# Order of two attentions in an encoder layer, and attention scores on row halves

## The chip, the cores and the metric

One core of a Trainium2 chip runs the whole kernel. The metric is the device time of one execution in microseconds. TensorE (PE) does the matrix products and transposes, its weight loads stand apart as PEld, VectorE is DVE, ScalarE is ACT, GpSimd is POOL, SyncE (SP) issues the transfers.

## The reference

One hybrid encoder layer on 256 rows of width 2048, all in fp32. A vector `c` gives shift, scale and gate for a mixer and a feed-forward part (`mod = silu(c) @ w_ada`). The mixer projects the modulated norm of x once; its columns feed two groups of eight heads, whose outputs are concatenated and projected.

```python
# differential attention: two maps of 64 per head, values of 128
s = einsum('bqhcd,bkhcd->bhcqk', q * 64 ** -0.5, k)
p = softmax(s)
out_d = einsum('bhqk,bkhe->bqhe', p[:, :, 0] - lam * p[:, :, 1], v)   # then RMSNorm per head
# latent attention: q and (k, v) projected up from latents of 512 and 256
s = (einsum('bqhd,bkhd->bhqk', q_nope, k_nope)        # 128 per head
     + einsum('bqhr,bkr->bhqk', q_rope, k_rope)) * 192 ** -0.5   # 64, one key for all heads
out_m = einsum('bhqk,bkhe->bqhe', softmax(s), v)
x = x + gate * (concat(out_d, out_m) @ w_out)
```

The feed-forward part (hidden width 8192, squared ReLU) and a last norm follow; the change leaves both as they are.

## The kernel before

**Products.** Every weight of the projections is loaded as fp32 in pieces of 128 rows by 1024 columns and split into two fp32r tiles: `split` casts the high half on ACT (L123) and subtracts it on DVE for the low half (L124). A product is then three matmuls (high by high, high by low, low by high) of 512 columns in `block` (L309). Raw weights have a ring of five buffers, their halves one of four. Scores, probabilities and transposes are single fp32 products.

**Modulation.** `w_ada` is applied on the side, in units: DVE multiplies a piece into an accumulator, two steps per MB (L376); some pieces go to PE instead, as four column tiles (L392). A run of the program takes a given number of units (the table `NA_`).

**Streams.** The program is written as generators, and `run` interleaves them by the weights of the table `RW`; a scheduler then fixes the order of each engine, which runs its instructions in that order. PSUM has eight banks: four for the projections ("mm"), a ring of three for attention ("at"), one for the gate groups.

**Order around the change.** The input projection ends with a last group of four k-tiles in four parts (latents, values, queries, keys of the differential heads). Beside its last two parts runs the first head pair's latent projection (`latent_kv`, L552 `pk` and `pv`; `latent_q`, `pq` and `pr`, with a swap product for the rotary halves). Then comes `attention`, alone with 18 units of modulation: for each head the latent scores (`ms`), the differential heads' transposes (`dT`, L664) and scores (`ds`, L677), and two heads later the transposes of the probabilities (`mtp`, `dtp`) and the outputs (`mo`, `do`). Then follow the latent half of the output projection's first 1024 columns with four units, the norm of the differential heads (`diff_norm`, L710 to L718: clamp, square, row sum, product) and their transposes (`oT`, L725), the differential half (`od`) of these columns, and the second 1024 columns.

**Scores.** A head's two maps of 64 rows share the 128 partitions. The keys are copied into a tile with zeros in the other half (`kz`), so that one 128-row product of 512 columns gives both maps' scores for 128 queries. The latent rotary part has its keys zero-padded in the same way (`krz`). Scores go into "mm" banks. The softmax takes the row maximum on DVE (L603), scales it (L604), and exponentiates on ACT with the scale (L606); reciprocals of the row sums multiply the probabilities.

Of the kernel before, what the change touches and what calls it, by code (L numbers as in the profile page):

```python
# [11 lines left out]
F32 = mybir.dt.float32  # L12
# [43 lines left out]
NA_ = (0, 2, 5, 18, 4, 2, 0)  # L56
PRI_ADA = 0
RW = (11.9, 5.6, 0.5, 2.88, 1.44, 28.56, 13.6, 6.8, 336.0, 45.0, 42.0, 3.53, 60.48, 6.0)
FW = (42.0, 2.0, 2, 2)
PRI_ATT = 0  # L60

TWO_PI = 2.0 * np.pi
# [22 lines left out]
def encoder_layer(ctx: ExitStack, tc: tile.TileContext, x, c, positions, w_ada, b_ada, g_norm_mix, w_in,  # L85
# [41 lines left out]
    def splits(w, raw, name, ext):  # L127
        if not ext:
            return [split([P, w], raw[:, i, :], f"{name}{i}") for i in range(2)]
        hi = act.tile([P, 2, w], F32R, tag="n0", name=name + "_hi")  # L130
        lo = act.tile([P, 2, w], F32R, tag="n1", name=name + "_lo")
# [364 lines left out]
    krz = mla_g[:, 512:1024].rearrange("p (a q) -> p a q", a=2)  # L496
# [11 lines left out]
    def latent_prep():  # L508
        g.memset(krz, 0.0)
# [33 lines left out]
        v.tensor_tensor(krz[0:64, 0, :], t1[0:64, :], t2[0:64, :], ALU.add)  # L543
        v.tensor_tensor(krz[64:128, 1, :], t1[64:128, :], t2[64:128, :], ALU.add)
# [10 lines left out]
    def latent_kv(hp):  # L555
# [8 lines left out]
        s.copy(kn[hp % 2], pk.rearrange("p (h q) -> p h q", h=2))  # L564
# [9 lines left out]
    def latent_q(hp, hold):  # L574
# [24 lines left out]
        hold.append((qn, qr))  # L599

    def softmax_rows(sc, scale, p, sums, name):
        nm = small.tile([P, 2], F32, tag="nm", name=name + "_nm")
        v.tensor_reduce(nm, sc, AX.X, ALU.max, negate=True)  # L603
        v.tensor_scalar(nm, nm, scale, None, op0=ALU.mult)  # L604
        for i in range(2):
            s.activation(p[:, i, :], sc[:, i, :], AF.Exp, bias=nm[:, i:i + 1], scale=scale,  # L606
                         accum_out=sums[:, i:i + 1])
        v.reciprocal(sums, sums)

    def latent_scores(h, qn, qr):  # L610
        i = h % 2
        kh = kn[h // 2 % 2][:, i, :]
        sc = bank(f"ms{h}", "mm")
        for t in range(T):
            pe.matmul(sc[:, t * S:(t + 1) * S], lhsT=qn[:, i, t * P:(t + 1) * P], rhs=kh, start=True, stop=False)
            pe.matmul(sc[:, t * S:(t + 1) * S], lhsT=qr[:, t * P:(t + 1) * P], rhs=krz[:, i, :],
                      start=False, stop=True)
        p = p_buf()
        sums = small.tile([P, 2], F32, tag="sums", name=f"msum{h}")
        softmax_rows(sc.rearrange("p (t k) -> p t k", t=2), float((NOPE + ROPE) ** -0.5), p, sums, f"m{h}")  # L620
        for t in range(T):
            s.mul(p[:, t, :], p[:, t, :], sums[:, t:t + 1])
        return p
# [36 lines left out]
    def diff_heads_T(h):  # L660
# [5 lines left out]
        qT = at.tile([P, S], F32, tag="dqT", name=f"dqT{h}", bufs=2)  # L666
        s.copy(qT, pt[:, 0:S])
        z = kz[h % 2]
        s.copy(z[0:64, 0, :], pt[0:64, S:2 * S])
        v.tensor_copy(z[64:128, 1, :], pt[64:128, S:2 * S])  # L670
        return qT, z

    def diff_scores(h, qT, z):
        ps = []
        for t in range(T):
            sc = bank(f"ds{h}{t}", "mm")
            pe.matmul(sc, lhsT=qT[:, t * P:(t + 1) * P], rhs=z.rearrange("p a b -> p (a b)"), start=True, stop=True)  # L677
            p = p_buf()
            sums = small.tile([P, 2], F32, tag="sums", name=f"dsum{h}{t}")
            softmax_rows(sc.rearrange("p (t k) -> p t k", t=2), float(DH ** -0.5), p, sums, f"d{h}{t}")  # L680
            v.tensor_tensor(sums[:, 1:2], sums[:, 1:2], nlam, ALU.mult)
            s.mul(p[:, 0, :], p[:, 0, :], sums[:, 0:1])
            v.scalar_tensor_tensor(p[:, 0, :], p[:, 1, :], sums[:, 1:2], p[:, 0, :], op0=ALU.mult, op1=ALU.add)
            ps.append(p)
        return ps
# [363 lines left out]
```

## Time and profile before

| | us |
|---|---|
| median of 3 runs (lowest, highest) | 1185.48 (1183.98, 1187.21) |
| the profiled execution | 1184.91 |
| its span | 1183.1 |
| PE busy in the span | 1139.7 (96%) |
| DVE busy | 810.0 (68%) |
| ACT busy | 552.4 (47%) |
| POOL busy | 53.3 (5%) |

The span is what the profiler saw, the time includes what lies around it. Busy shares are means over stages that differ: the attention stage lies between about 226 and 372 us, where single fp32 products and small steps take the place of long rows of fp32r products. A busy time per instruction can overlap the next one's on PE, so a price is better read from start to start. The mean granted clock of TensorE in this execution is .993 of 2.4 GHz.

### The profile page before, as it was taken

To read this page: it belongs to the slowest core of one execution; us is meant where nothing else is said; L and a number is where in the kernel's file an instruction comes from. 1 tells how busy PE (TensorE), PEld (TensorE's weight loads), DVE (VectorE), ACT (ScalarE), POOL (GpSimd) and SP (SyncE) were. 2 spreads that over 40 slices of the span, in tenths; PEclk is the share of its full clock that TensorE was granted. 3 is DMA by queue.
4 is the path that set the end of the run, shared out by engine and by line. 5 is a ranking of instruction groups with operands and counts; after the bars stand their busy time and mean duration, and the time that the engine had idled before them with its cause. 6 is when DMAs were issued, how large, how long until landed. Compare 5 with 4: busy or idle time off the path is not lost.

```text
span 1183.1 us, 14211 instructions
## 1 busy us (share of the span) xinstructions
PE 1139.7 (96%) x5502; PEld 913.8 (77%) x5502; DVE 810.0 (68%) x1012; ACT 552.4 (47%) x811; POOL 53.3 (5%) x50
## 2 busy tenths in 40 slices
PE   5999999998999998999999999999999999999996
PEld 4566778865778886888888888888888888888875
DVE  3245559996899869775754666676686676555776
ACT  3432334547774436545545444344344344344343
POOL 1000000112101000000000000000020002000000
PEclk9999999999999999999999999999999999999999
DMA  9999974786788877995565646667868767556531
GB/s 347 393 390 369 359 302 131 258 308 215 294 307 300 300 276 275 356 329 194 184 225 179 204 158 207 232 236 263 278 220 277 280 241 249 183 181 203 183 104 72
DMA packets 94196, 297.50 MB, mean 251 GB/s; under 512 B 5712, under 2 KB 16167, under 8 KB 93488
## 3 DMA queue, kind: packets, MB, share of 16 engines
q1 hardware_dynamic: 94016, 296.56, 71.3%
q8 instruction: 43, 0.70, 0.2%
q14 instruction: 25, 0.20, 0.0%
q10 hardware_dynamic: 112, 0.03, 0.0%
HBM read 294.47 MB, written 2.10 MB: 251 GB/s over the span
## 4 chain that ended last, share of the span: by engine, by line
PE 59%; DVE 1%; issue 1%; ACT 0%; ACTq 0%; POOLq 0%; POOL 0%
PE f_p L309 51%; PE f1a_p L309 7%; PE fT L936 1%; DVE x_res L954 0%; DVE acc L953 0%; DVE acc L951 0%; PE shift_f_pc L417 0%; PE scale_f_pc L417 0%; PE h2T L889 0%; ACT acc L885 0%; DVE acc L957 0%; ACT sq L960 0%; PE h2a L858 0%; ACT h2a10t L831 0%; ACT acc L981 0%
## 5 line engine op out<-in xcount | busy, mean ns | idle before, releaser
L124 DVE TENSOR_TENSOR f_w_lo<-f_r,f_w_hi 128x1024 fp32r<-128x1024 f32 x224 | 277.2, 1245 | 200.9 <-ACT f_w_hi L123 200.8
L123 ACT CAST f_w_hi<-f_r 128x1024 fp32r<-128x1024 f32 x224 | 236.2, 1054 | 317.6 <-PE f_p L309 300.3
L309 PE MATMUL f_p<-f_w_hi,h 128*128 128x512 f32 x768 | 209.5, 391 | 0.0
L309 PEld LDWEIGHTS f_p<-f_w_hi,h 128*128 128x128 f32 x768 | 143.4, 188 | 29.3 <-ACT h L892 0.2
L309 PE MATMUL f_p<-f_w_lo,fh 128*128 128x512 f32 x512 | 158.9, 389 | 0.0
L309 PE MATMUL f_p<-f_w_hi,fh 128*128 128x512 f32 x512 | 158.5, 390 | 0.3 <-ACT fh L938 0.3
L309 PE MATMUL f_p<-f_w_hi,fl 128*128 128x512 f32 x512 | 158.7, 389 | 0.0
L309 PE MATMUL in_p<-in_w_hi,hT 128*128 128x512 f32 (+1 forms) x512 | 140.8, 388 | 4.6 <-ACT hT L364 2.8
L309 PE MATMUL f_p<-f_w_lo,h 128*128 128x512 f32 x384 | 118.9, 390 | 0.0
L309 PEld LDWEIGHTS in_p<-in_w_hi,hT 128*128 128x128 f32 x512 | 95.0, 189 | 29.0 <-ACT in_w_hi L123 6.3
L309 PEld LDWEIGHTS f_p<-f_w_hi,fh 128*128 128x128 f32 x512 | 96.0, 188 | 21.6 <-DVE acc L951 1.2
L309 PEld LDWEIGHTS f_p<-f_w_hi,fl 128*128 128x128 f32 x512 | 96.0, 188 | 20.0
L309 PEld LDWEIGHTS f_p<-f_w_lo,fh 128*128 128x128 f32 x512 | 96.1, 188 | 19.7
L124 DVE TENSOR_TENSOR in_w_lo<-in_r,in_w_hi 128x1024 fp32r<-128x1024 f32 (+1 forms) x64 | 73.2, 1169 | 45.1 <-ACT in_w_hi L123 44.9
L309 PEld LDWEIGHTS f_p<-f_w_lo,h 128*128 128x128 f32 x384 | 72.0, 188 | 14.8
L309 PE MATMUL in_p<-in_w_lo,hT 128*128 128x512 f32 (+1 forms) x256 | 78.8, 386 | 1.7 <-DVE in_w_lo L124 1.5
L123 ACT CAST in_w_hi<-in_r 128x1024 fp32r<-128x1024 f32 (+1 forms) x64 | 62.8, 1010 | 37.0 <-PE in_p L309 27.4
L309 PE MATMUL f1a_p<-f1a_w_hi,h 128*128 128x512 f32 x256 | 69.4, 391 | 3.0 <-ACT h L863 3.0
L309 PEld LDWEIGHTS f1a_p<-f1a_w_hi,h 128*128 128x128 f32 x256 | 47.8, 188 | 14.0 <-ACT h L863 3.9
L309 PEld LDWEIGHTS in_p<-in_w_lo,hT 128*128 128x128 f32 x256 | 47.7, 189 | 12.2 <-DVE in_w_lo L124 5.1
L123 ACT CAST out_w_hi<-out_r 128x1024 fp32r<-128x1024 f32 x30 | 31.6, 1052 | 35.7 <-PE out_p L309 35.7
L376 DVE SCALAR_TENSOR_TENSOR gate_f<-gate_f_r,cs,gate_f 128x1024 f32<-128x1024 f32 x32 | 40.9, 1280 | 7.0 <-DMA gate_f_r<-w_ada 6.9
(341 smaller groups left out, 1374.9 us busy)
## 6 DMA issues: line engine op xcount, KB each, us to landing
f_r<-w_ff SPq DMA_DIRECT2D x112, 1024.0 KB, 5.6
in_r<-w_in SPq DMA_DIRECT2D x24, 1024.0 KB, 9.9
sc__r<-w_ada SPq DMA_DIRECT2D x16, 1024.0 KB, 12.1
sh__r<-w_ada SPq DMA_DIRECT2D x16, 1024.0 KB, 13.4
gate_m_r<-w_ada SPq DMA_DIRECT2D x16, 1024.0 KB, 6.8
scale_f_r<-w_ada SPq DMA_DIRECT2D x16, 1024.0 KB, 8.0
out_r<-w_out SPq DMA_DIRECT2D x16, 1024.0 KB, 7.6
shift_f_r<-w_ada SPq DMA_DIRECT2D x16, 1024.0 KB, 7.9
```

Of the source, the lines that this page charges most:

```text
L123: s.copy(hi, src)
L124: v.tensor_tensor(lo, src, hi.bitcast(F32), ALU.subtract)
L309: pe.matmul(ps[t][j][:, 0:nw], lhsT=lhs[(lk0 + kk) // 8][:, (lk0 + kk) % 8, t * P:(t + 1) * P], rhs=rhs[:, n0:n0 + nw], start=(kk == 0 and ...
L376: v.scalar_tensor_tensor(acc, raw[:, i, :], cs[:, k + i:k + i + 1], acc, op0=ALU.mult, op1=ALU.add)
L936: pe.transpose(pt[:, i * S + t * P:i * S + (t + 1) * P], rl[:, t, (kp + i) * P:(kp + i + 1) * P], ident)
```

## The change

- Latent attention of all four head pairs (`latent_attention`, with a pair's output one pair later) runs beside the last two parts of the input projection, with 17 units of modulation.
- Differential attention (`diff_attention`) runs beside the latent half of the output projection's first 1024 columns, with 5 units. The norm is split in two halves of four heads: the first stands behind head 3's output, within that stage, the second behind the stage. The split results `od` get tiles of their own, and the residual's rows are loaded earlier.
- Scores are products of 64 rows: the two heads of a latent pair and the two maps of a differential head take partitions 0 to 63 and 64 to 127 of the same tiles, with no zero padding. A differential head issues four products of 256 columns in place of two of 512. Scores go into the ring of three banks.
- The softmax scale is folded into the copies of keys and queries. The first map's row sum is kept (`s0_all`) and put into the norm, instead of dividing each map.

```diff
-NA_ = (0, 2, 5, 18, 4, 2, 0)
+NA_ = (0, 2, 17, 5, 0, 2)
...
-        s.copy(kn[hp % 2], pk.rearrange("p (h q) -> p h q", h=2))
+        s.mul(kn[hp % 2], pk.rearrange("p (h q) -> p h q", h=2), MLA_SCALE)
...
+    def softmax_rows(sc, p, sums, name):
         nm = small.tile([P, 2], F32, tag="nm", name=name + "_nm")
         v.tensor_reduce(nm, sc, AX.X, ALU.max, negate=True)
-        v.tensor_scalar(nm, nm, scale, None, op0=ALU.mult)
...
+    def latent_scores(hp):
+        qn, qr = hold[hp]
+        scs = [bank(f"ms{2 * hp + i}") for i in range(2)]
+        for t in range(T):
+            for i in range(2):
+                hs = slice(64 * i, 64 * i + 64)
+                pe.matmul(scs[i][:, t * S:(t + 1) * S], lhsT=qr[hs, t * P:(t + 1) * P], rhs=kr[hs, :],
+                          start=True, stop=False)
+            for i in range(2):
+                pe.matmul(scs[i][:, t * S:(t + 1) * S], lhsT=qn[:, i, t * P:(t + 1) * P], rhs=kn[hp % 2][:, i, :],
+                          start=False, stop=True)
...
+    def diff_scores(h, qkT):
+        scs = [bank(f"ds{h}{c_}") for c_ in range(2)]
+        for t in range(T):
+            for c_ in range(2):
+                hs = slice(64 * c_, 64 * c_ + 64)
+                pe.matmul(scs[c_][:, t * S:(t + 1) * S], lhsT=qkT[hs, 0, t * P:(t + 1) * P], rhs=qkT[hs, 1, :],
+                          start=True, stop=True)
+        ps = [p_buf(), p_buf()]
+        s0 = s0_all[:, h, :]
+        s1 = small.tile([P, 2], F32, tag="sums", name=f"dsum{h}")
+        for c_, sm in enumerate((s0, s1)):
+            softmax_rows(scs[c_].rearrange("p (t k) -> p t k", t=2), ps[c_], sm, f"d{h}{c_}")
+        v.reciprocal(s1, s1)
+        v.scalar_tensor_tensor(s1, s1, nlam, s0, op0=ALU.mult, op1=ALU.mult)
+        for t in range(T):
+            v.scalar_tensor_tensor(ps[0][:, t, :], ps[1][:, t, :], s1[:, t:t + 1], ps[0][:, t, :],
+                                   op0=ALU.mult, op1=ALU.add)
...
-    def diff_norm():
-        for t in range(T):
-            o_ = qk[t][:, 0:1024]
+    def diff_norm(part):
+        hs = slice(part * HQ, (part + 1) * HQ)
+        for t in range(T):
+            o_ = qk[t][:, part * 512:(part + 1) * 512]
...
+    def latent_attention():
+        for hp in range(H // 2 + 1):
+            if hp < H // 2:
+                yield from latent_kv(hp)
+                yield from latent_q(hp)
+            for h in (2 * hp - 2, 2 * hp - 1):
+                if h >= 0:
+                    lT = latent_probs_T(h, lps[h])
+                    yield 0.5
+                    latent_out(h, lT)
+                    yield 1.0
+            if hp < H // 2:
+                yield from latent_scores(hp)
+
+    run((RW[5], chain(in_block(gl, 2), diff_rope(0), in_block(gl, 3), diff_rope(1))), (RW[6], latent_attention()),
+        (RW[7], take(ada_m, NA_[2])))
...
+    def diff_attention():
+        live = {}
         for i in range(H + LAG):
             if i < H:
+                live[i] = diff_scores(i, diff_heads_T(i))
                 yield 2.0
             if i >= LAG:
+                diff_out(i - LAG, diff_probs_T(i - LAG, live.pop(i - LAG)))
+                yield 1.5
+            if i - LAG == HQ - 1:
+                yield from diff_norm(0)
...
-    run((42.0, take(out0, H // 2)), (RW[11], take(ada_m, NA_[4])))
-    run((1.0, diff_norm()))
-    xt = load_x("x_res", XQ)
+    run((RW[8], take(out0, 3)), (RW[9], diff_attention()), (RW[10], take(ada_m, NA_[3])))
+    run((1.0, diff_norm(1)))
```

On DVE, from the first pair's key and value weights on, before (`kv0_lo` is the low half of the first pair's weights, `in3_0_w` are weights of the input projection, `q0_0_lo` and `q0_1_lo` those of the first pair's queries, `gate_m0` a modulation step, `qk0` a sum of the input projection):

```order
L124 TENSOR_TENSOR kv0_lo_1793<-kv_r0_1790,kv0_hi_1792 128x1024
L376 SCALAR_TENSOR_TENSOR gate_m0_1672<-gate_m0_r4_1810,cs_82,gate_m0_1672 128x1024
L124 TENSOR_TENSOR in3_0_w20_lo_1835<-in3_0_r2_1832,in3_0_w20_hi_1834 128x1024
L376 SCALAR_TENSOR_TENSOR gate_m0_1672<-gate_m0_r6_1828,cs_82,gate_m0_1672 128x1024
L124 TENSOR_TENSOR in3_0_w21_lo_1839<-in3_0_r2_1832,in3_0_w21_hi_1838 128x1024
L376 SCALAR_TENSOR_TENSOR gate_m0_1672<-gate_m0_r6_1828,cs_82,gate_m0_1672 128x1024
L124 TENSOR_TENSOR q0_0_lo_1873<-q_r0_1870,q0_0_hi_1872 128x768
L465 TENSOR_TENSOR qk0_91<-in3_0_p00_1762,qk0_91 128x512
L465 TENSOR_TENSOR qk0_91<-in3_0_p01_1763,qk0_91 128x512
```

In this row of before the pair's query weights stand behind six other steps, and the latent scores come only in the next run. The same place after the change, up to the rotated query (`qr0`) of the first scores:

```order
L124 TENSOR_TENSOR kv0_lo_1794<-kv_r0_1791,kv0_hi_1793 128x1024
L376 SCALAR_TENSOR_TENSOR gate_m0_1671<-gate_m0_r4_1811,cs_82,gate_m0_1671 128x1024
L124 TENSOR_TENSOR q0_0_lo_1832<-q_r0_1829,q0_0_hi_1831 128x768
L124 TENSOR_TENSOR q0_1_lo_1836<-q_r0_1829,q0_1_hi_1835 128x768
L376 SCALAR_TENSOR_TENSOR gate_m0_1671<-gate_m0_r6_1856,cs_82,gate_m0_1671 128x1024 x2
L376 SCALAR_TENSOR_TENSOR gate_m0_1671<-gate_m0_r8_1888,cs_82,gate_m0_1671 128x1024 x2
L124 TENSOR_TENSOR kv1_lo_1931<-kv_r1_1928,kv1_hi_1930 128x1024
L376 SCALAR_TENSOR_TENSOR gate_m0_1671<-gate_m0_r10_1924,cs_82,gate_m0_1671 128x1024
L504 TENSOR_TENSOR qr0_r1_1893<-pr0_1873,trig_86 128x256
L505 TENSOR_TENSOR qr0_r2_1894<-pr0_1873,trig_86 128x256
L376 SCALAR_TENSOR_TENSOR gate_m0_1671<-gate_m0_r10_1924,cs_82,gate_m0_1671 128x1024
L597 TENSOR_TENSOR qr0_1892<-qr0_r1_1893,qr0_r2_1894 128x256
```

The query weights moved ahead of four modulation steps and of the weights of the second pair; one modulation step stands right ahead of the rope products and one between them and their sum.

On PE, at the first half of the norm, after the change (`do3` is head 3's output, `out0` the projection with the latent half `om` as its other operand, `oT0` and `oT1` the transposes behind the norm, `dT6` those of head 6):

```order
L707 MATMUL do3_2913<-dv1_94,pT12_2907 128x128
L309 MATMUL out0_p11_2637<-out0_w61_hi_3168,om00_1749 128x512
L309 MATMUL out0_p10_2636<-out0_w61_lo_3169,om00_1749 128x512
L309 MATMUL out0_p11_2637<-out0_w61_lo_3169,om00_1749 128x512
L309 MATMUL out0_p10_2636<-out0_w61_hi_3168,om01_1750 128x512
L309 MATMUL out0_p11_2637<-out0_w61_hi_3168,om01_1750 128x512
L742 MATMUL oT0_2956<-ident_70,qk0_91 128x128
L742 MATMUL oT1_2963<-ident_70,qk0_91 128x128
L668 MATMUL dT6_2970<-ident_70,qk0_91 128x128
L742 MATMUL oT0_2956<-ident_70,qk1_92 128x128
L742 MATMUL oT0_2956<-ident_70,qk0_91 128x128
L742 MATMUL oT0_2956<-ident_70,qk1_92 128x128
```

Before, the transposes of the norm stood behind the whole latent half of the projection; here five of its products lie between head 3's output and them, and what follows them in the projection has `od` as its operand.

On DVE, from the row sums of that half norm to its two products (L735; `qk0_91` and `qk1_92` hold the outputs, `shift_f0` is a modulation step):

```order
L732 TENSOR_SCALAR z200_2928<-z200_2928 128x4
L728 SCALAR_TENSOR_TENSOR dms01_2946<-z201_2944,dms01_2946 128x4
L376 SCALAR_TENSOR_TENSOR shift_f0_3200<-shift_f0_r6_3317,cs_82,shift_f0_3200 128x1024
L733 TENSOR_TENSOR fin00_2935<-dss00_2926,z200_2928 128x4
L732 TENSOR_SCALAR z201_2944<-z201_2944 128x4
L376 SCALAR_TENSOR_TENSOR shift_f0_3200<-shift_f0_r8_3382,cs_82,shift_f0_3200 128x1024
L734 TENSOR_TENSOR dr00_2933<-dr00_2933,fin00_2935 128x4
L733 TENSOR_TENSOR fin01_2951<-dss01_2942,z201_2944 128x4
L376 SCALAR_TENSOR_TENSOR shift_f0_3200<-shift_f0_r8_3382,cs_82,shift_f0_3200 128x1024
L735 TENSOR_TENSOR qk0_91<-qk0_91,dr00_2933 128x512
L734 TENSOR_TENSOR dr01_2949<-dr01_2949,fin01_2951 128x4
L735 TENSOR_TENSOR qk1_92<-qk1_92,dr01_2949 128x512
```

Three modulation steps stand within these rows; the clamps (L720) and sums (L723) stand right ahead of them, with one low half of output weights and a fourth modulation step between. In the order before such steps lay among the steps of the whole norm too, with the projection's latent half on PE beside them.

## Rows read from the trace of the kernel before

**Rows 1.** Windows: PE, PEld, DVE, ACT, POOL busy by stretch; PEclk, DMA share, GB/s.
```profile
225.96:399.94 173.98, 166.33 (x902) 127.75 (x900) 153.23 (x265) 106.66 (x260) 20.95 (x10) 0.98 0.83 294
...
225.96:251.00 25.04, 24.80 (x139) 21.52 (x138) 24.93 (x38) 9.13 (x14) 0.00 (x0) 1.00 0.93 335
...
251.00:346.00 95.00, 88.13 (x508) 61.74 (x507) 79.51 (x165) 71.14 (x205) 15.25 (x7) 0.98 0.78 270
...
399.94:460.00 60.06, 56.68 (x261) 45.67 (x259) 48.11 (x56) 32.19 (x55) 2.85 (x3) 1.00 0.72 259
...
270.00:280.00 10.00, 10.00 (x63) 6.39 (x61) 5.95 (x13) 8.36 (x24) 0.00 (x0) 0.85 0.80 269
```

**Rows 2.** Timeline, PE: start, us, line, op, out<-in, xcount, [idle before].
```profile
225.96 0.40 PE L552 MATMUL pk<-cq,kv_hi 128*128 128x256 f32 x2
...
226.19 0.28 PE L552 MATMUL pk<-cq,kv_lo 128*128 128x256 f32 x1
...
252.31 0.59 PE L616 MATMUL ms<-mla_g,qr 128*128 128x256 f32 x2
...
252.84 1.06 PE L392 MATMUL gate_m_pg<-gate_m_r,cpad 128*32 128x512 f32 x8
...
253.83 0.51 PE L552 MATMUL pk<-cq,kv_hi 128*128 128x256 f32 x2
```

**Rows 3.** Timeline, PE: one head pair's round of the old attention.
```profile
287.65 0.59 PE L616 MATMUL ms<-mla_g,qr 128*128 128x256 f32 x2
...
288.08 0.60 PE L629 MATMUL mtp<-ident,asc 128*128 128x128 f32 x4
...
288.52 0.60 PE L664 MATMUL dT<-ident,qk 128*128 128x128 f32 x4
...
292.62 1.98 PE L677 MATMUL ds<-asc,dqT 128*128 128x512 f32 x4
...
294.44 1.05 PE L700 MATMUL do<-dv,pT 128*128 128x128 f32 x8
...
295.25 0.48 PE L552 MATMUL pk<-cq,kv_hi 128*128 128x256 f32 x2
```

**Rows 4.** Timeline, PE: a wait, the old norm's transposes, the stretch's end.
```profile
269.17 0.38 PE L552 MATMUL pq<-cq,q_lo 128*128 128x256 f32 x1 [3.12 <-DVE q_lo L124]
...
374.08 1.07 PE L725 MATMUL oT<-ident,qk 128*128 128x128 f32 x8
...
399.48 0.62 PE L309 MATMUL out_p<-out_w_hi,od 128*128 128x512 f32 x2
...
399.94 0.62 PE L309 MATMUL out_p<-out_w_hi,om 128*128 128x512 f32 x2
```

**Rows 5.** Timeline, DVE: steps of one stretch.
```profile
223.69 1.23 DVE L124 TENSOR_TENSOR kv_lo<-kv_r,kv_hi 128x1024 fp32r<-128x1024 f32 x1
...
224.83 1.28 DVE L376 SCALAR_TENSOR_TENSOR gate_m<-gate_m_r,cs,gate_m 128x1024 f32<-128x1024 f32 x1
...
226.03 1.22 DVE L124 TENSOR_TENSOR in_w_lo<-in_r,in_w_hi 128x1024 fp32r<-128x1024 f32 x1
...
230.69 0.95 DVE L124 TENSOR_TENSOR q_lo<-q_r,q_hi 128x768 fp32r<-128x768 f32 x1
...
304.59 0.41 DVE L505 TENSOR_TENSOR qr_r<-pr,trig 128x256 f32<-128x256 f32 x1
...
308.89 0.69 DVE L603 TENSOR_REDUCE m_nm<-ms 128x2 f32<-128x512 f32 x1
...
310.09 0.16 DVE L604 TENSOR_SCALAR m_nm<-m_nm 128x2 f32<-128x2 f32 x1
```

**Rows 6.** Timeline, ACT: an exponential of a softmax.
```profile
310.43 0.48 ACT L606 ACTIVATE asc<-ms,m_nm 128x256 f32<-128x256 f32 x1
```

**Rows 7.** Timeline, DVE: the old norm, first clamp and last product.
```profile
355.40 0.68 DVE L710 TENSOR_SCALAR qk<-qk 128x1024 f32<-128x1024 f32 x1
...
370.87 1.22 DVE L718 TENSOR_TENSOR qk<-qk,dr_rs 128x1024 f32<-128x1024 f32 x1
```

More of the change, by code (lines that the diff above doesn't have):

```diff
@@ L598, in latent_q @@
         v.tensor_tensor(qr, t1, t2, ALU.add)
[L599 to L601 removed]
+        hold[hp] = (qn, qr)
+    def softmax_rows(sc, p, sums, name):
         nm = small.tile([P, 2], F32, tag="nm", name=name + "_nm")
         v.tensor_reduce(nm, sc, AX.X, ALU.max, negate=True)
[L604 removed]
         for i in range(2):
[L606 removed]
+            s.activation(p[:, i, :], sc[:, i, :], AF.Exp, bias=nm[:, i:i + 1], scale=1.0,
@@ L607, in softmax_rows @@
                          accum_out=sums[:, i:i + 1])
[L608 to L613, printed above, removed]
-        for t in range(T):
[L615 to L620, printed above, removed]
-        for t in range(T):
-            s.mul(p[:, t, :], p[:, t, :], sums[:, t:t + 1])
-        return p
+    def latent_scores(hp):
+        qn, qr = hold[hp]
+        scs = [bank(f"ms{2 * hp + i}") for i in range(2)]
+        for t in range(T):
+            for i in range(2):
[5 more added lines that the diff above has]
+                          start=False, stop=True)
+        for i in range(2):
+            h = 2 * hp + i
+            p = p_buf()
+            sums = small.tile([P, 2], F32, tag="sums", name=f"msum{h}")
+            softmax_rows(scs[i].rearrange("p (t k) -> p t k", t=2), p, sums, f"m{h}")
+            v.reciprocal(sums, sums)
+            for t in range(T):
+                s.mul(p[:, t, :], p[:, t, :], sums[:, t:t + 1])
+            lps[h] = p
+            yield 1.4
@@ L665, in diff_heads_T, with diff_probs_T @@
                              qk[t][:, o * 1024 + h * P:o * 1024 + (h + 1) * P], ident)
[L666 to L674, printed above, removed]
-        for t in range(T):
[L676 to L685, printed above, removed]
-    def diff_probs_T(h, ps):
+        qkT = qkT_ring[h % 2]
+        s.mul(qkT[:, 0, :], pt[:, 0:S], float(DH ** -0.5))
+        s.copy(qkT[:, 1, :], pt[:, S:2 * S])
+        return qkT
+    def diff_scores(h, qkT):
+        scs = [bank(f"ds{h}{c_}") for c_ in range(2)]
+        for t in range(T):
+            for c_ in range(2):
[12 more added lines that the diff above has]
+                                   op0=ALU.mult, op1=ALU.add)
+        return ps[0]
+    def diff_probs_T(h, p):
         tp = bank(f"dtp{h}")
@@ L773, in encoder_layer @@
     om_hi, om_lo = pair("om", (0,))
[L774 to L782 removed]
+    hold, lps = {}, {}
+    s0_all = at.tile([P, H, T], F32, name="s0_all")
+    p_ring = [lat[t][:, 0:512].rearrange("p (a q) -> p a q", a=2) for t in range(T)]
+    p_ring.append(at.tile([P, 2, S], F32, tag="px", name="px"))
     cnt = {"p": 0, "pT": 0}
@@ L820, in encoder_layer @@
+    xt = load_x("x_res", XQ)
     x1_sums = row_sums("x1s")
@@ L866, in encoder_layer @@
     run((42.0, chain(out0, mixer_out(1024, mix_lhs, x1_sums, mid=lambda: h2_first(0)))),
-        (RW[13], chain(ada_m, take(ada_l, 1), flush(), take(ada_l, NA_[5]))))
+        (RW[11], chain(ada_m, take(ada_l, 1), flush(), take(ada_l, NA_[5]))))
     h2_first(1)
```

82 lines of the change are left out of this document (31 added, 51 removed).

## The prediction

> **What bounds the kernel now.** I read the windows first, then PE's timeline in order of time, then DVE's and ACT's steps in it. Ahead of 225.96 us, and from the first matmul of the projection's second half (399.94) on, the change leaves the order of the instructions nearly as it was; what it moves lies in the 173.98 us between them. PE is busy for 166.33 of these, DVE for 153.23, ACT for 106.66 [rows 1]. So PE sets the time, but DVE is close: it is full in the first 25 us (24.93 of 25.04, with DMA at .93) and has room afterwards (79.51 of 95.00) [rows 1]. PE's timeline gives the pitch of each kind of work, from start to start: an fp32r product of 512 columns .23 us (.46 for two) [rows 4], of 256 columns .12 [rows 2], an fp32 product of 256 columns .43 and a transpose .11 (.44 for four), an old differential score of 512 columns .91, one head's four output products .81 [rows 3]. A gate group (four column tiles of 512 fp32 columns, shown as 8) takes .99, little more than one such product alone, with .10 ahead of it [rows 2]. (An fp32 product stands there as two records, an fp32r product as one.)
>
> PE's own work there: in-block 72 x .23 = 16.6; latent projections 240 x .12 = 28.8; 52 fp32 products of 256 columns (32 scores, 16 outputs, 4 swaps) 22.4; 16 old differential scores 14.6; 112 transposes 12.3; eight output heads 6.5; eight gate groups with their ends about 10.7; the projection's 192 x .23 = 44.2; the column sums 1.7 (between the end of DVE's last product, 372.1 [rows 7], and the transposes at 374.08 [rows 4], less .3). Together 157.8, so 16.2 of the 173.98 are waits and slow clock. The largest single wait is 3.12 at 269.17 [rows 4]; in the 10 us after it the granted clock is .85 [rows 1], which at half speed for the missing part is 1.5 us lost.
>
> **The change, part by part.**
>
> Scores on row halves. The latent rope parts fall from 16 products to 8 pairs: 8 x .43 = 3.4 saved if the two of a pair run side by side. The differential scores fall from 14.6 to 17 x .43 = 7.3 (16 pairs; one is split by the order), 7.3 saved. No row shows row halves. The nearest is the gate group, whose column tiles overlap [rows 2]: so I take full overlap. Leaving and entering that group costs .10 + (.99 - .86) = .23, say .24; with 16 visits to the halves (two per latent pair, one per differential head) 3.8. Taken: -3.4 - 7.3 + 3.8 = **-6.9**; bounds -10.7 (switching free) and +3.0 (no overlap: 23 more products of .43, 9.9). The Trainium skill's page "TensorE: Matmul & The Clock Gate", section "Measured speedup vs the span model", gives 3.07 for four row tiles, so one pass takes about 1.3 of a product; by it the sum would be an estimated 3 us higher, and no run here shows it. The Trainium skill's page "TensorEngine Tiling (Array Packing)", section "Key Properties", says that a change of tiling mode drains the engine, which speaks against the change; the .24 around column tiles agrees with it [rows 2].
>
> Fewer steps on DVE and ACT (the scale folded into copies, the first map's row sum moved into the norm): about 10 us less on DVE and 6 on ACT. I count nothing: neither is the bound on average, and what the steps could shorten is in the waits below.
>
> The old waits go with the old order: **-16.2**. Its norm took DVE from 355.40 to 372.1 [rows 7], but PE ran the projection's latent half meanwhile, so its removal gives nothing.
>
> New waits, walked through the new order of each engine. DVE prices: low half of a split 1.14, modulation step 1.20, rope product .4, q_lo .86, reduce .6, small step .1 or so [rows 5].
> - First latent pair: after its low half DVE has a modulation step, two q_lo, four modulation steps, the next pair's low half, another step, two rope products, another step, then the sum that the first score needs: 223.69 + 1.14 + 1.20 + 1.72 + 4.80 + 1.14 + 1.20 + .8 + 1.20 + .4 = 237.3. PE has its 60 products and the swap behind it at 225.96 + 7.2 + 1.0 = 234.2. Wait 3.1.
> - In-block weights behind the first pair's softmax on ACT: 1.9; swaps and probability copies of later pairs: 1.5. Both are estimates from ACT steps of .48 [rows 6].
> - A differential head's scores take two of the three banks of the ring, and the next user waits for a reduce, two exponentials and an ACT copy of 512 columns, .6 + 2 x .48 + .6 = 2.2; transposes .44 and four projection products .9 cover 1.3. Six heads x .9 = 5.4.
> - First half norm: between head 3's output and the transposes PE has only five projection products, 1.1; the latent half is then used up. DVE's chain is: two half clamps .7 (half of [rows 7]), head 5's two combines .8, two reduces 1.2, a low half 1.14, four modulation steps 4.8, twelve small steps 1.2, two half products 1.2 (half of [rows 7]): 11.0. Wait 9.9. Behind it in PE's order stand head 6's transposes and scores, the projection's differential half and the outputs of heads 4 and 5; DVE and ACT, with nothing of head 6 done, then cost about 3 more.
> - Second half norm: the same without modulation steps and combines, 5.4, and ACT's and POOL's steps in it, some 2.7: 8.1, of which 18 projection products cover 4.1. Wait 4.0.
>
> Together 3.1 + 1.9 + 1.5 + 5.4 + 9.9 + 3.0 + 4.0 = **+28.8**; bounds: 14 (each wait halved because the steps run ahead) and 36 (DMA late too). The clock: after three waits of 3 us or more it falls as at 270 to 280, 3 x 1.5 = **+4.5**; bounds 0 and 6.
>
> Transfers: the same bytes, spread further (DMA share .93 in the first 25 us, .78 in the next 95 [rows 1]): 0. On SP's queue the two loads of the residual now stand ahead of the third and fourth pair of output weights, and wait there for the latent tiles to come free; two earlier pairs of weights cover that. Without this cover 2 MB at 294 GB/s [rows 1] are 7 us of that queue. DVE's modulation steps done earlier shorten nothing later: the projection's second half has PE at 56.68 of 60.06 and DVE at 48.11 [rows 1].
>
> Sum: -6.9 - 16.2 + 28.8 + 4.5 = +10.2. The profiled execution took 1184.91 us, .57 under the median of the runs (1185.48): 1184.91 + 10.2 = **1195**. With A's own bounds it lies in 1187 to 1202.
>
> **The rivals.**
>
> B, faster: DVE runs ahead. Place: DVE's queue at the first half norm. In each of the waits for score banks DVE too is idle, waiting for ACT, and may spend that on the low half and the four modulation steps that I laid into the chain (5.9), whose data come by DMA. Then the wait is 4.0, the 3.0 behind it, the second norm's 4.0 and half of the bank waits (2.7) go, and two of three clock dips: -5.9 - 9.7 - 3.0 = -18.6, 1176.5. It decides by whether DVE reaches the first clamp when ACT has just written head 3. For it: DVE's 15 us of room between 251 and 346 [rows 1]. Against it: these steps stand behind the clamps in DVE's order.
>
> C, no change: only the overlap of waits holds (the 9.7), the chain stays: 1185.4.
>
> D, slower: the change doesn't do what it says, row halves run one behind the other. Place: the 8 rope pairs and 15 of the score slots; price 23 x .43 = 9.9: 1205.0. Against it: the column tiles overlap [rows 2].
>
> **How the numbers follow.** A .48, B .16, C .24, D .12. About .3% (3.6 us) is what a measurement can tell from no change: faster means under 1181.9, slower over 1189.1. A and D are slower, .60; B is faster, .16; C's own width of some 5 us puts a third of it under the limit (.08) and leaves .16 the same: faster .24, same .16, slower .60. The range leaves out about half of B below and, with waits longer than forecast, half of D above: 1177 to 1206. A's own, 1187 to 1202, stands beside it.
>
> **What would show it.** In the profile after: two ds records of a head starting within .1 us and four taking about .9 (not 1.7); PE idle some 10 us ahead of the oT transposes of the first half norm, released by DVE's product, with shift_f steps between clamp and product on DVE; a wait of about 3 us ahead of the first score, released by qr; a granted clock below .9 after these waits. The forecast is wrong if PE's wait ahead of the transposes is under 5 us, or if the waits named sum to under 18.

## The result and the profile after

The changed kernel takes 1202.24 us (median of 4 runs, 1200.42 to 1204.99); the kernel before, run beside it, 1185.88 (median of 4). The ratio is 1.0141 [1.0126, 1.0157]: slower by 16.4 us, or by 15.5 between the two profiled executions (1200.42 against 1184.91). The forecast was +10.2, at 1195; the result lies in its range of 1177 to 1206, at the upper end of A's own (1187 to 1202). The profiled execution is the shortest of the four, at a mean granted clock of .988 where the others have .983 to .986, so that the clock's part below is read low.

The windows of the kernel after, first the stretch from the first product of the first pair's weights to the first product of the projection's second half (189.84 us; before it was 173.98 [rows 1]), then the stretch that the ledger below uses, and 5 us behind the longest wait:

```profile
224.94:414.78 189.84, 170.22 (x934) 125.41 (x932) 147.65 (x240) 101.46 (x244) 22.25 (x10) 0.95 0.77 272
225.00:430.00 205.00, 185.38 (x1001) 137.95 (x1000) 161.17 (x253) 110.03 (x257) 22.25 (x10) 0.95 0.76 268
370.00:375.00 5.00, 3.98 (x17) 3.31 (x19) 3.25 (x7) 1.93 (x4) 0.00 (x0) 0.57 0.94 347
```

PE is idle 19.62 of 205.00 us, at a granted clock of .95. Before, in the same stretch:

```profile
225.00:430.00 205.00, 197.35 (x1046) 153.66 (x1046) 178.79 (x288) 122.14 (x280) 21.91 (x11) 0.98 0.82 296
```

That is 7.65 idle at .98. PE's waits of the kernel after in this stretch (who waits, for whom: total, times, longest):

```profile
PE oT L742 <- DVE dr L734: 10.8, 1, 10.8
PE ms L613 <- DVE qr L597: 3.2, 1, 3.2
PE oT L742 <- DVE qk L735: 2.9, 1, 2.9
PE dT L668 <- ACT asc L604: 0.9, 3, 0.5
PE mtp L633 <- ACT lat L625: 0.7, 1, 0.7
PE pr L593 <- ACT mla_g L592: 0.5, 1, 0.5
```

Three waits make 16.9 of the 19.62: ahead of the first half norm's transposes, ahead of the first latent scores, ahead of the second half norm's transposes. The places on PE's timeline, with the idle time ahead and its releaser in brackets; the rows at 254.91 and 257.81 are gate groups of one product and of four (to the next start .97 and 1.00), those from 288.10 to 290.43 the scores of a latent pair (L613 the row halves, two pairs of products; L616 four whole products), those at 331.09 and 355.43 the four scores of heads 1 and 5:

```profile
236.65 0.70 PE L613 MATMUL ms<-mla_g,qr 64*128 64x256 f32 x4 [3.19 <-DVE qr L597]
...
254.91 1.04 PE L392 MATMUL gate_m_pg<-gate_m_r,cpad 128*32 128x512 f32 x2
255.88 0.70 PE L593 MATMUL pr<-mla_g 128*128 128x256 f32 x2
...
257.81 1.06 PE L392 MATMUL gate_m_pg<-gate_m_r,cpad 128*32 128x512 f32 x8
258.81 0.48 PE L641 MATMUL mo<-pT,mla_f 128*128 128x256 f32 x1
...
288.10 0.70 PE L613 MATMUL ms<-mla_g,qr 64*128 64x256 f32 x4
288.74 1.13 PE L616 MATMUL ms<-mla_f,mla_g 128*128 128x256 f32 x4
289.80 0.70 PE L613 MATMUL ms<-mla_g,qr 64*128 64x256 f32 x4
290.43 1.13 PE L616 MATMUL ms<-mla_f,mla_g 128*128 128x256 f32 x4
291.49 1.06 PE L392 MATMUL gate_m_pg<-gate_m_r,cpad 128*32 128x512 f32 x8
...
331.09 2.29 PE L680 MATMUL ds<-asc 64*128 64x256 f32 x8
333.31 0.66 PE L668 MATMUL dT<-ident,qk 128*128 128x128 f32 x4
...
355.43 1.13 PE L680 MATMUL ds<-asc 64*128 64x256 f32 x8
356.50 0.65 PE L699 MATMUL dtp<-ident,asc 128*128 128x128 f32 x4
...
371.02 0.66 PE L742 MATMUL oT<-ident,qk 128*128 128x128 f32 x2 [10.83 <-DVE dr L734]
...
397.68 0.44 PE L742 MATMUL oT<-ident,qk 128*128 128x128 f32 x2 [2.90 <-DVE qk L735]
...
414.78 0.62 PE L309 MATMUL out_p<-out_w_hi,om 128*128 128x512 f32 x2
```

Before, the same transposes had no row of a wait ahead of them [rows 4]. What DVE did during the 10.83, on its timeline from the half norm's first clamp on:

```profile
360.87 0.41 DVE L720 TENSOR_SCALAR qk<-qk 128x512 f32<-128x512 f32 x1
...
362.45 1.27 DVE L723 TENSOR_REDUCE dss<-qk 128x4 f32<-128x512 f32 x2
...
363.70 1.22 DVE L124 TENSOR_TENSOR out_w_lo<-out_r,out_w_hi 128x1024 fp32r<-128x1024 f32 x1
...
364.98 1.28 DVE L376 SCALAR_TENSOR_TENSOR shift_f<-shift_f_r,cs,shift_f 128x1024 f32<-128x1024 f32 x1
...
369.00 1.27 DVE L376 SCALAR_TENSOR_TENSOR shift_f<-shift_f_r,cs,shift_f 128x1024 f32<-128x1024 f32 x1
...
370.99 0.69 DVE L735 TENSOR_TENSOR qk<-qk,dr 128x512 f32<-128x512 f32 x1
```

The chain is the forecast's: clamps, head 5's two combines, sums, one low half, four modulation steps (364.98, 366.32, 367.66, 369.00) with the small steps between them, products, back to back. Behind the wait the granted clock is .57 (window 370 to 375).

**The ledger.** For each kernel I split 225 to 430 us three ways: idle is 205 less PE's busy time; clock loss is, summed over windows of 1 us, PE's busy time times the missing part of the granted clock; what is left of the profiled time is called work (it holds everything outside the stretch too, idle time and slow clock included).

| kernel | profiled us | idle | clock loss | work |
|---|---|---|---|---|
| before | 1184.91 | 7.65 | 3.24 | 1174.0 |
| after | 1200.42 | 19.62 | 6.67 | 1174.1 |
| difference | +15.5 | +12.0 | +3.4 | +.1 |

The slowdown is idle time and slow clock. The work, which the row halves were to shorten by 6.9, is what it was.

### The profile page after: what moved, and what is told of

It reads as the page before. It is cut to its first block, busy times and chain, and to the rows that moved or that the text cites. A ratio compares the mean times of both kernels' runs of the same rounds, so it can differ in the third digit from the quotient of the medians.

```text
span 1198.6 us, 14242 instructions
## 1 busy us (share of the span) xinstructions
PE 1144.8 (96%) x5534; PEld 912.5 (76%) x5534; DVE 806.7 (67%) x987; ACT 547.6 (46%) x798; POOL 54.1 (5%) x49
## 4 chain that ended last, share of the span: by engine, by line
PE 57%; DVE 1%; issue 1%; ACT 1%; DMA 0%; ACTq 0%; POOLq 0%; POOL 0%
PE f_p L309 49%; PE f1a_p L309 7%; PE fT L954 1%; DMA gate_f_r<-w_ada 0%; DVE acc L969 0%; DVE x_res L972 0%; DVE acc L971 0%; PE shift_f_pc L417 0%; PE scale_f_pc L417 0%; PE h2T L907 0%; DVE gate_f L376 0%; ACT acc L903 0%; DVE acc L975 0%; ACT sq L978 0%; DVE f_w_lo L124 0%
## 5 line engine op out<-in xcount | busy, mean ns | idle before, releaser
L123 ACT CAST f1a_w_hi<-f1a_r 128x1024 fp32r<-128x1024 f32 x30 | 31.5, 1054 | 28.1 <-PE f1a_p L309 28.1
```

The costliest lines, as they stand in the source:

```text
L123: s.copy(hi, src)
```

## The experiments

Each is one edit of the changed kernel, or of the version of e3. In most of them the question is the same: does a wait that is taken away give its time back, or does it come back at another place? The expectations state the theories of each run.

**e1: both half norms behind the stage.**

```diff
-            if i - LAG == HQ - 1:
-                yield from diff_norm(0)
...
-    run((1.0, diff_norm(1)))
+    run((1.0, chain(diff_norm(0), diff_norm(1))))
```

> The changed kernel with both half norms behind the differential stage, nothing else moved. Theory A (the first half norm's chain stands on TensorE's path with nothing to cover it): the wait of 10.8 us ahead of the first transposes of the norm falls under 1, since four heads' norm now has the last four heads' work in front of it; the half-speed stretch and the 3 us behind the wait go too; ahead of the second transposes a wait of 2 to 4 stays. Time 1202 - 10.8 - 3 = 1186 to 1190. Theory B (VectorE's work in that stage is the bound, and the wait is only where it shows): the wait comes back ahead of other instructions, and the time stays over 1197.

Measured: 1194.0 (ratio 1.0068 [1.0051, 1.0085]), 8.2 less than after and between the times of the two theories. Idle fell from 19.62 to 11.35, and the wait ahead of the transposes to .85, as A says. But the output products of the last heads now wait for their probabilities, and one stretch lost its clock:

```profile
367.09 2.07 PE L707 MATMUL do<-dv,pT 128*128 128x128 f32 x8 [3.07 <-ACT pT L700]
```

```profile
365.00:390.00 25.00, 20.04 (x81) 16.53 (x82) 19.79 (x49) 11.32 (x35) 3.41 (x4) 0.59 0.57 194
```

PE is busy for 20.04 of 25 us there at a granted clock of .59, most of it at the lower of the two levels (1.2 GHz); the clock loss is 11.57 (after: 6.67). So the norm's place makes the wait, and in this execution more than half of the idle time taken away comes back as clock. It is the longest of e1's four (1198.72; the others 1191.76 to 1194.34), at a mean granted clock of .984 where they have .987 to .992: how much comes back differs from one execution to the next.

**e2: the first half norm's steps put ahead of what is queued.**

```diff
-                yield from diff_norm(0)
+                yield from prio(60, diff_norm(0))
```

> The changed kernel with the first half norm's steps put ahead of others by priority: two of the four modulation steps leave the stretch between clamp and product on VectorE, all else stays. Theory A: the wait of 10.8 us falls by the two steps, 2 x 1.2, to 8.4, and the time by the same 2.4 to about 1199.8. Theory B: the steps only stand elsewhere, the next waits grow by as much, and the time stays at 1202.

Measured: 1206.82 (1.0181 [1.0165, 1.0196]), 4.6 more than after. PE's timeline, then DVE's in the second half norm:

```profile
370.47 2.05 PE L742 MATMUL oT<-ident,qk 128*128 128x128 f32 x8 [8.52 <-DVE qk L735]
...
401.30 2.14 PE L742 MATMUL oT<-ident,qk 128*128 128x128 f32 x8 [6.05 <-DVE qk L735]
```

```profile
397.82 1.28 DVE L376 SCALAR_TENSOR_TENSOR shift_f<-shift_f_r,cs,shift_f 128x1024 f32<-128x1024 f32 x1
...
399.17 1.28 DVE L376 SCALAR_TENSOR_TENSOR shift_f<-shift_f_r,cs,shift_f 128x1024 f32<-128x1024 f32 x1
```

The first wait fell by 2.3, as both theories have it; the time came out above both. Two modulation steps came back in the chain of the second half norm, whose wait grew from 2.90 to 6.05. DVE's steps are only moved, and the wait with them, at a higher price: clock loss is 10.14 (after: 6.67).

**e3: the order of before, with the row halves, the folded scale and the kept row sums.** It takes the order part of the change back (attention of both kinds together, the norm behind the projection's latent half, scores in the projections' banks).

```diff
-NA_ = (0, 2, 17, 5, 0, 2)
+NA_ = (0, 2, 5, 18, 4, 0, 2)
...
+    run((RW[8], attention()), (RW[9], take(ada_m, NA_[3])))
...
+    run((42.0, take(out0, H // 2)), (RW[10], take(ada_m, NA_[4])))
+    run((1.0, chain(diff_norm(0), diff_norm(1))))
```

> The order of the kernel before (both attentions together, the projection's latent half over the norm), with the scores on row halves, the folded scale and the row sums of the change. Theory A (the row halves save what their shorter products say, and only the order costs): 10.7 saved less 16 switches of .21 = 7.3, so about 1178.5 against 1185.9 before. Theory B (that stage's ends are set by VectorE and ScalarE, not by the scores): 1183 to 1187. Theory C (row halves cost more than they save): over 1189.

Measured: 1185.71, ratio 1.0005 [.9994, 1.0016]: the time of before. Work fell by 4.4 (to 1169.6), idle rose to 10.28 and clock loss to 5.65. So, with the row halves in both, the whole +16.4 lies in what this run takes back, and the halves bring nothing on their own here: what PE saves returns as waits and slow clock. The run takes back the place of both attentions, the norm's place, the scores' banks and the units of modulation together; it doesn't tell them apart. Its largest wait, and a window:

```profile
PE mo L641 <- ACT pT L635: 4.5, 1, 4.5
```

```profile
300.00:346.00 46.00, 39.47 (x242) 28.56 (x243) 44.14 (x69) 28.37 (x84) 5.97 (x3) 0.89 0.90 326
```

DVE is busy for 44.14 of 46 us there and the DMA share is .90: with less work on PE, DVE has next to no slack in that stretch (e8 tests it). Work holds one more fall of the clock, outside the ledger's stretch; before, the clock of the same 10 us is 1.00:

```profile
540.00:550.00 10.00, 9.79 (x51) 7.96 (x51) 5.83 (x11) 6.46 (x13) 0.95 (x1) 0.83 0.43 152
```

**e4: the two halves issued apart.** All products of the first map, then those of the second; do halves overlap only when neighbours in the order alternate?

```diff
-        for t in range(T):
-            for c_ in range(2):
+        for c_ in range(2):
+            for t in range(T):
```

> The changed kernel with the four products of a differential head issued map by map (two on rows 0 to 63, then two on rows 64 to 127) instead of in turn. In the changed kernel head 1 alone has this order, and its four take 2.22 us in place of 1.06. Theory A (two products of different rows overlap only as neighbours): the four take 2.2 in every head, seven heads by 1.16 more, and the time rises by up to 8, to 1206 to 1210. Theory B (head 1 was slow for another reason, such as a bank): 1.06 to 1.3 in the others, time within 1 of 1202.

Measured: a head's four scores take what they did (rows of heads 1 and 5):

```profile
332.59 2.28 PE L680 MATMUL ds<-asc 64*128 64x256 f32 x8
...
358.38 1.14 PE L680 MATMUL ds<-asc 64*128 64x256 f32 x8
```

The overlap doesn't need alternation. Head 1's row is long in either order, and the trace names the reason, a wait for a bank within the row: the second map's first product is released by an exponential of an earlier softmax (L604) and starts .04 behind its end in both runs (332.25 in after, 333.74 here). The time, 1206.82 (2 runs; 1.0182 [1.0162, 1.0203]), is no price of the edit: the order elsewhere came out differently (transposes wait 10.06 and 4.31, clock loss 9.06).

**e5: the `shift_f` steps to PE**, as column groups, out of DVE's chain.

```diff
-EARLY_PE = (False, False)
+EARLY_PE = (False, True)
```

> The changed kernel with the first eight units of shift_f (those that run beside the differential attention) as column tiles on TensorE instead of 16 steps of 1.2 us on VectorE. Theory A (the modulation steps in the norm's chain make the wait): no modulation step stands between clamp and product, the wait of 10.8 us falls to 5 or 6, and that ahead of the second half norm doesn't grow as it did when the steps were only put off; eight groups of about 1.0 us come on TensorE, some of them inside the wait; time 1196 to 1199. Theory B (the wait moves to whatever is next): 1202 or more.

Measured: 1201.94 (1.0156 [1.0134, 1.0178]), as after. The wait fell as the chain did, the one ahead of the second half norm didn't grow (.58), and the time is still not A's. PE's timeline, and from the lines view what PE got for it:

```profile
367.58 0.44 PE L742 MATMUL oT<-ident,qk 128*128 128x128 f32 x2 [4.11 <-DVE qk L735]
```

```profile
L392 PE MATMUL shift_f_pg<-shift_f_r,cpad 128*32 128x512 f32 x64 | 9.8, 614 | 0.7 <-ACT shift_f L397 0.7
```

Idle fell by 8.5 and clock loss by 2.1; work rose by 12.0. That settles that the modulation steps in the chain made the larger part of the wait (10.83 to 4.11), and that PE has no room for them either.

**e6: fewer modulation steps beside the first pair.**

```diff
-RW = (11.9, 5.6, 0.5, 2.88, 1.44, 21.2, 54.0, 17.0, 15.6, 29.0, 5.0, 8.5)
+RW = (11.9, 5.6, 0.5, 2.88, 1.44, 21.2, 54.0, 8.0, 15.6, 29.0, 5.0, 8.5)
```

> The changed kernel with the modulation's weight beside the latent attention lowered from 17 to 8, so that fewer of its steps stand ahead of the first pair's rotated query on VectorE. Theory A (the 3.2 us wait ahead of the first scores comes from these steps, and the half-speed stretch behind it from the wait): both go, 4.5 us, time 1197 to 1198. Theory B (steps put off come back in the differential stage, where VectorE is full): the wait goes, later waits grow by as much, 1202.

Measured: 1213.64 (1.0253 [1.0236, 1.0270]), the slowest of all.

```profile
235.91 0.70 PE L613 MATMUL ms<-mla_g,qr 64*128 64x256 f32 x4 [0.38 <-DVE qr L597]
...
409.90 0.69 PE L742 MATMUL oT<-ident,qk 128*128 128x128 f32 x2 [10.14 <-DVE qk L735]
```

The first pair's wait is gone (3.19 to .38), so the forecast's account of it holds. The steps put off come later. The first half norm's wait falls to 4.0, but the second half norm, which waited 2.90, now waits 10.14, and six waits for ACT ahead of the differential scores make 6.7 more; idle 26.19, clock loss 15.91. That is B's return of the steps, at several times its price.

**e7: the first half norm one head later.**

```diff
-            if i - LAG == HQ - 1:
+            if i - LAG == HQ - 1 + 1:
```

> The changed kernel with the first half norm one head later (behind head 4's output instead of head 3's). Theory A (what counts is what TensorE has to do between head 3's output and the transposes): head 6's transposes and scores and head 4's output, 2.8 us more, stand there, the wait falls to about 8, and the differential half of the projection still covers the last heads, as it does not with the norm at the end (1194); time 1190 to 1198. Theory B: VectorE's work is the bound and the wait only shifts: over 1200.

Measured: 1202.03 (1.0155 [1.0138, 1.0172]), as after and as B says. Idle fell by 6.3 and clock loss rose by 6.1:

```profile
365.00:390.00 25.00, 19.81 (x85) 15.34 (x86) 18.78 (x37) 9.85 (x30) 2.10 (x2) 0.66 0.58 193
```

One wait of 10.83 became two of 3 (an output 3.06, the transposes 3.03), and around them the clock was low for longer.

**e8: e3 with modulation on PE.** If DVE bounds e3, taking its steps should free the time that the halves saved.

```diff
-EARLY_PE = (False, False)
+EARLY_PE = (True, False)
```

> The order of the kernel before with row halves (1185.7), and the first eight units of scale_f as column tiles on TensorE instead of 16 steps of 1.2 us on VectorE. Theory A (in the old order the row halves' gain went into waits for VectorE, which was busy for 44 of 46 us from 300 to 346): VectorE has 19 us less, TensorE 9 us more in groups that partly fall into its waits; time 1179 to 1184. Theory B (TensorE is the bound after all): 1190 to 1195.

Measured: 1192.62 (1.0074 [1.0054, 1.0094]). Idle 7.60 and clock loss 1.71, both less than e3's by 2.7 and 3.9, but work 16.0 more. In e3's full stretch DVE has less than half of its work left, and PE hardly waits:

```profile
300.00:346.00 46.00, 45.05 (x290) 28.59 (x287) 20.26 (x58) 28.07 (x92) 5.28 (x3) 1.00 0.59 203
```

So DVE's steps did make the waits there, as A says, but the time is B's: the column groups cost PE more than the waits did.

**e9: useless products ahead of the first half norm's transposes**, so that PE isn't idle there.

```diff
+        if part == 0:
+            fl = bank("fill", "gv")
+            for _ in range(8):
+                pe.matmul(fl, lhsT=ident, rhs=qk[1][:, 1024:1536], start=True, stop=True)
```

> The changed kernel with eight products of no use (.91 us each, 7.3 us in all, from the squares of the first half norm into a bank that nobody reads) on TensorE between the five projection products and the transposes of the first half norm, so that TensorE works through most of its 10.8 us wait. Theory A (the granted clock falls because TensorE idles): the wait falls to about 3, the transposes still start where they did, the granted clock of the 5 us behind them stays over .9 instead of .57, and the stretch from the transposes to head 6's scores takes 1.5 us less; time 1200 to 1202. Theory B (the clock falls for another reason, such as what runs behind the wait): the clock behind the wait is as low as before and nothing is gained.

Measured: 1208.93 (3 runs; 1.0200 [1.0176, 1.0225]). The useless products fill most of the wait, the transposes start at 371.53 (after: 371.02), and the second half norm waits longer:

```profile
363.10 7.13 PE L740 MATMUL fill<-qk,ident 128*128 128x512 f32 x16 [2.30 <-ACT qk L721]
...
371.53 0.44 PE L746 MATMUL oT<-ident,qk 128*128 128x128 f32 x2 [1.29 <-DVE qk L735]
...
402.00 2.15 PE L746 MATMUL oT<-ident,qk 128*128 128x128 f32 x8 [7.76 <-DVE qk L735]
```

The clock behind the first wait:

```profile
370.00:375.00 5.00, 3.71 (x20) 2.43 (x19) 3.53 (x6) 1.81 (x4) 0.00 (x0) 1.00 0.97 365
```

1.00 where after has .57: the idle time ahead drops the clock. The whole is slower by 6.7. The order of the instructions behind the place came out differently, the second half norm waits 7.76 instead of 2.90, and the clock falls there (clock loss 8.14 in all). So what idle time does to the clock is shown at the place, and no gain in time.

**e10: e3 with its modulation earlier; e11: e3 with the second head's softmax issued later**, both aimed at e3's waits.

```diff
-RW = (11.9, 5.6, 0.5, 2.88, 1.44, 28.56, 13.6, 6.8, 336.0, 45.0, 3.53, 6.0)
+RW = (11.9, 5.6, 0.5, 2.88, 1.44, 28.56, 13.6, 6.8, 336.0, 64.0, 3.53, 6.0)
```

> The order of the kernel before with row halves, and the modulation's weight beside the attention raised from 45 to 64, so that its steps come earlier, where VectorE had room (275 to 305 us: busy 15 of 30) and fewer stand where it was full (325 to 345). Theory A (VectorE's full stretch caused the waits that took the row halves' gain): idle time of TensorE in 225 to 430 us falls from 10.3 to about 7, its clock loss from 5.7 to about 3; time 1179 to 1182, faster than both. Theory B (the steps only collide elsewhere): 1184 to 1188.

```diff
-                yield from latent_scores(i // 2)
+                second = latent_scores(i // 2)
+                yield next(second)
+            elif i < H:
+                yield from second
```

> The order of the kernel before with row halves, with the softmax of a latent pair's second head one head later, as in the kernel before, where each head's scores came by themselves. Theory A (a pair's eight steps at once on ScalarE hold the copies of transposed probabilities up: the 4.5 us wait at 340 us): that wait falls by about 2, and the clock behind it with it; time 1181 to 1184. Theory B (VectorE is what is late there): 1185 to 1187.

Measured: e10 1189.22 (1.0030 [1.0019, 1.0040]), with its largest wait 4.19; e11 1188.23 (1.0025 [1.0013, 1.0038]), with e3's wait of 4.50 cut to 3.35. Neither beats e3, and both are above the times of their two theories. In e10 clock loss fell by 2.4, but idle rose by 1.5 and work by 2.9. In e11 idle and clock loss fell by 3.4 together, but work came out 7.0 higher. Of that 3.9 is idle time (2.7) and clock loss (1.2) behind the ledger's stretch, from 430 us on; the rest stays open.

**e12: e1 with useless products ahead of the outputs of heads 4 to 7** (three for head 4, one for each other: seven of .91, 6.4 us).

```diff
+                p = live.pop(i - LAG)
+                dT = diff_probs_T(i - LAG, p)
+                if i - LAG >= HQ:
+                    fl = bank(f"fill{i}", "gv")
+                    for _ in range(3 if i - LAG == HQ else 1):
+                        pe.matmul(fl, lhsT=ident, rhs=p.rearrange("p a b -> p (a b)"), start=True, stop=True)
+                diff_out(i - LAG, dT)
```

> The kernel with both half norms behind the differential stage (1194.0), and products of no use (.91 us each, from a head's probabilities into a bank that nobody reads) between the transposes and the outputs of heads 4 to 7: three for head 4, where TensorE waited 3.07 us, one each for the others. The order that comes of it also leaves nine of the projection's products for heads 6 and 7. Theory A (in that kernel 20 us of the last heads ran at half the clock because TensorE had idled ahead of them, and this ate what the later norm gave back): clock loss from 11.6 to under 5, the granted clock from 365 to 390 over .9, time 1184 to 1189. Theory B (the last heads are as slow as VectorE and ScalarE let them be): the clock may stay up, but the waits grow, and the time stays at 1192 or more.

Measured: 1189.79 (6 runs; 1.0046 [1.0027, 1.0066]), with 6.4 us more for PE to do than in e1. The medians differ by 4.2, but the intervals overlap (e1: [1.0051, 1.0085]), so that it is faster than e1 is not shown; that it isn't slower by its 6.4 us is.

```profile
365.00:390.00 25.00, 24.10 (x131) 18.07 (x130) 24.27 (x56) 15.29 (x40) 6.71 (x4) 1.00 0.56 199
```

The clock is 1.00 where e1 has .59, clock loss 2.98 (e1: 11.57), idle 6.34 (11.35): theory A's clock, at a time just above its range. This compares with e1's longest execution; the mean granted clock of e12's six is .991 to .993, of e1's four .984 to .992. Part of the idle time saved, and so of the clock, comes from the order, which left nine projection products for heads 6 and 7; how much is not told apart. No version beats the kernel before.

## Why the prediction was right in its sign and short in its size

- **The first half norm.** Forecast 9.9, measured 10.83, with the chain on DVE as written. e5 shows the modulation steps in it to be its larger part. Rival B, that DVE runs ahead of the chain, fell: the low half and the four modulation steps ran between the clamps and the products.
- **The first pair.** Forecast 3.1, measured 3.19, released by `qr`; e6 removes it by removing the steps.
- **The second half norm.** Forecast 4.0, measured 2.90.
- **Bank waits.** Forecast 5.4 for six heads; the waits that PE shows for ACT around the differential scores (`dT`, `do`) are 1.2, and head 1's row adds 1.15 within (2.22 to the next start, where the others take 1.07). Too much by about 3. The 3 behind the half norm left no wait of that size either. In-block and swap waits: forecast 3.4, measured 1.2 (`mtp` .7, `pr` .5).
- **The clock.** Forecast +4.5 beside the 1.5 at 270 that the old waits' 16.2 held; measured 6.67 in all, 3.24 before. The clock falls behind all three waits, as forecast (.72 in 236 to 242, .57 in 370 to 375, .69 in 395 to 406); in the kernel before it falls twice too (at 270 [rows 1] and .66 in 375 to 380), and the forecast missed the second time.
- **The old waits, -16.2.** Idle and clock loss of before are 10.9 (7.65 + 3.24). The 5.3 over were work that I had priced too low and so credited to the change as waits.
- **Waits and clock together**: the forecast's net was +17.1 (28.8 + 4.5 - 16.2), the ledger's +15.4. Right in sum, by errors that offset: the new waits and their clock came out 7.0 lower than forecast (26.3 for 33.3), the old ones 5.3. That is luck. Rival C, by which the waits cancel, fell.
- **The step that failed: "scores on row halves", -6.9.** The ledger has +.1, 7.0 more; less the 1.7 above, that is the 5.3 by which the profiled execution exceeds 1195.
  - The overlap is full, and rival D fell: a head's four scores take 1.07 to the next start with .09 ahead, 1.16 against 1.82 for the two old ones [rows 3], so -5.3 for eight.
  - But "switching 16 times at .24" was too cheap at the latent pairs. There whole fp32 products stand on both sides, and a visit costs .40: .09 in the product ahead, .20 on leaving, .10 in the first product behind. In the rows from 288.10 on this is .63 for a pair of halves (.43 + .20) and 1.06 for the two products behind it (.86 + .20). A latent pair's scores take 3.39 from 288.10 to 291.49, .10 of it for the gate group behind [rows 2], so 3.3 against 8 x .43 = 3.46 before: -.7 for four pairs, where the forecast had -1.5.
  - Then two terms that I had not written down. Head 1's wait inside its row is +1.15. And the new order splits the eight gate groups over 13 visits, where before had 9; a visit of one product takes .97 and one of four 1.00, so that 13 take 12.81 from start to start and 9 took 9.9 (10.78 less .87 for one at half clock): +2.9.
  - Together -5.3 - .7 + 1.15 + 2.9 = -1.95, so 2 us more were to be found. The traces place most of them. Counted from start to start, at full clock and without idle time, the projection's 193 products take 48.5 us after and 44.15 before: they stand in 29 pieces between attention's steps instead of 6. Less the .7 of entering the halves, counted above, and less 2.05 that the transposes `dT` and `dtp` next to them take less (6.35 for 8.4), that is +1.6. That the splitting is its cause is argued, not shown by an edit of its own.
  - e3, with 7 visits to the gate groups (9.55), should have -5.3 - .7 - .4 = -6.4, and its ledger has -4.4. The same count within its moved stretch gives 156.9 for 162.9, so -6.0; most of the rest is the fall of the clock at 540 to 550, outside the stretch.

On the overlap, the Trainium skill's page "TensorE: Matmul & The Clock Gate", section "Measured speedup vs the span model", gives a measured speedup of 3.07 for four row tiles, from which the prediction worked out an estimate of 1.3 products for a pass. The trace doesn't agree with that for two halves: two passes take .86 plus the switching, .43 each, the price of a single product. It is nearer to the model in the same section, by which each further tile adds only about 4 ns: the halves' starts lie 6 to 7 ns apart. The Trainium skill's page "TensorEngine Tiling (Array Packing)", section "Key Properties", says that a change of tiling mode drains the engine. The trace agrees: .09 on entering the halves, .20 on leaving.

Why the change as a whole costs time is shown by e3 (all of it lies in the order part of the change, which that run takes back) and by e1 (half of it, 8.2 of 16.4, goes with the norm's place). What e1 keeps above before is mostly clock in its profiled execution, 11.57 against 3.24; no run takes that half apart further. The old order had the projection's latent half over the norm; the new one spends that half beside the differential heads, and has five products left when the norm comes. DVE has no slack to give: a step put off returns in the next chain (e2, e6), a step given to PE costs PE as much or more (e5, e8), a wait split into smaller ones loses by the clock what it saves in idle time (e7). Only moving the norm behind gave time back (e1, and e12, which keeps PE busy there as well). One limit holds for all: a scheduler reorders everything behind an edit, so no run differs from its partner at one place alone; that is why e4 and e9 are read at their place and not by their time.

## What to carry to other kernels

Before a stage is moved, find what work stands over its dependent chain now, and count what will stand over it then: here the latent half of a projection had stood over the norm, five of its products were left, and the chain's length appeared on the path. Count a wait twice, as idle time and as slow clock behind it, and split the result into idle, clock and work before explaining it, since an expected saving can be missing in one while another looks right. When several engines are near full, price the return of a removed step at its next place before its removal.

## What was not expected of the hardware

- Row halves overlap fully in either order of issue (1.07 for four, e4), but entering them costs .09 and leaving them .20, and the first fp32 product behind takes .10 more; between single fp32 products they save next to nothing (3.3 against 3.46 at a latent pair).
- In e1 the granted clock was .59 over 25 us in which PE was busy for 20.04, with short fp32 products, transposes and gaps between them; with useless products in those gaps, and an order changed by them, it was 1.00, and the kernel with 6.4 us more for PE to do was no slower (e12).
- A column group's price hardly depends on how many of its four tiles are used: .97 for one, 1.00 for four.
